# The gate stores of the last built tile, issued on GpSimd's queue

## The chip, the cores and the metric

The kernel runs on one core of a Trainium2 chip. The metric is the device time of one launch in microseconds (us). PE is the matrix engine, DVE VectorE, ACT ScalarE, POOL GpSimd; SP is the engine that here only issues DMAs. Each engine runs its own list of instructions strictly in order; they meet through semaphores only. A DMA is issued by one engine, in that engine's order, and lands later.

## The reference, cut to what matters

One layer of an encoder trunk over 1024 tokens of width 1024, in float32: two kinds of attention, a projection, a layer norm, and then a PEER block, whose output goes through a second layer norm.

```
q   = x @ w_q                                  # 8 heads x 2 halves x 128
sc  = einsum(q, sub_keys)                      # 8 x 2 x 128 scores a token
s_top, i_top = top_k(sc, 16)                   # per half
cand = s_top[0][:, None] + s_top[1][None, :]   # 16 x 16 sums a head
fs, fpos = top_k(cand, 16)
eidx = the 16 expert numbers of a head (of 16384);  g = softmax(fs)
h   = x . u[eidx];   a = gelu(h) * g;   out = sum a * v[eidx]
```

So each token uses 128 experts of 16384, each with a gate g.

## The kernel before

Tokens stand in eight tiles (t = 0 to 7) of 128. Tiles 0 to 4 (`ND = 5`) are done densely: all 16384 experts are computed for them on PE, and a table of gates, mostly zeros, masks the result. Tiles 5 to 7 fetch the rows of their experts (`gather_gen`, L659, indirect DMAs on POOL).

The gate table of the dense tiles is made in two ways. For tiles 0 and 1 (`NS = 2`), `scatter` (L165) issues 256 indirect DMAs on POOL, each adding 128 gates into `gs` in DRAM. For tiles 2 to 4, `build` makes the table with one-hot products: for each of four quarters of 32 tokens there are eight steps, in each of which DVE compares (`pi` L605, `qj` L609), ACT scales `qj` by the gate (L614), PE multiplies (`pr`, L618) and ACT copies the product into the tile `stage` (L619). After eight steps the quarter, 2 MB, is stored to `gd` by one DMA (L620). The pool r1 holds `stage` with `bufs=1`: there is one buffer, and the first copy of a quarter waits until the store of the quarter before has landed.

The program is built in this order: projections, attention and `route(0)` (tiles 0 and 1, with all the scatters), then three rounds of attention of two tiles, with one `build(1)` after the attention of a tile while something is left to build, and `route(pr)`. `route` projects with w_q (16 steps c: loads `kt`, `qhi`, `qlo` on SP; PE `pq`; ACT copies `q` L562 and `sc` L567; DVE `top16`), and then `decode` on DVE finds expert numbers and gates. Tile 4 is routed in `route(2)`, so its build stands in the last round, after the attention of tile 6. The tile framework's scheduler then orders each engine's instructions by its own model of time; the four quarters of tile 4 come out interleaved with the steps of `route(3)` on ACT, DVE and PE.

After that the dense stage runs: 128 expert blocks e, with loads `gt` (gates, L703 from `gs` and L708 from `gd`), `raw` (L712, L730) on SP, the products `h` (L91 to L93), `po` and `fl` on PE, and the gathers of tiles 5 to 7 between them. The first `gt` load waits for every scatter and every store to `gd`.

Of the kernel before, what the change touches and what calls it, by code (L numbers as in the profile page):

```python
# [21 lines left out]
P = 128  # L22
# [15 lines left out]
ND = 5  # L38
NG = NT - ND
DN = ND * P  # L40
GC = 32
NS = 2
# [15 lines left out]
def trunk(ctx, tc, x, xt, wqk, wo, gn, sink, biasa, biasb, ln, wq, keyst, uv, ut, vt, out):  # L58
    nc = tc.nc
# [53 lines left out]
    gd = tc.dram_tile([(ND - NS) * P // GC, P, P, GC], F32, name="gd")  # L113
# [126 lines left out]
    with ExitStack() as att:  # L240
# [344 lines left out]
        def build(n):  # L585
            for t, idx, g in todo[:n]:
                ij = rb.tile([P, 2, P], F32, name="ij", bufs=1)
                tmp = rb.tile([P, 2, P], I32, name="ijt", bufs=1)
                nc.vector.tensor_scalar(tmp[:, 0, :], idx, 7, None, op0=OP.logical_shift_right)
                nc.vector.tensor_scalar(tmp[:, 1, :], idx, 127, None, op0=OP.bitwise_and)  # L590
                nc.vector.tensor_copy(ij, tmp)
                pt = ps_r.tile([P, 4, P], F32, name="pr")
                nc.tensor.transpose(pt[:, 0, :], ij[:, 0, :], ident)
                nc.tensor.transpose(pt[:, 1, :], ij[:, 1, :], ident)
                nc.tensor.transpose(pt[:, 2, :], g, ident)
                tt = rb.tile([P, 3, P], F32, name="tt", bufs=1)
                nc.scalar.copy(tt, pt[:, 0:3, :])
                for q in range(P // GC):
                    stage = r1.tile([P, P, GC], F32, name="stage")
                    for s in range(GC // 4):  # L600
                        ps = ps_r.tile([P, 4, P], F32, name="pr")
                        pi = rb.tile([P, 4, P], F32, name="pi")
                        tok0 = q * GC + s * 4
                        io4 = iota[:, None, :].to_broadcast([P, 4, P])
                        nc.vector.tensor_tensor(pi, io4, tt[:, 0, tok0:tok0 + 4, None].to_broadcast([P, 4, P]),  # L605
                                                OP.is_equal)
                        qj = rb.tile([P, 4, P], F32, name="qj")
                        if s % 4 < GACT:
                            nc.vector.tensor_tensor(qj, io4, tt[:, 1, tok0:tok0 + 4, None].to_broadcast([P, 4, P]),  # L609
                                                    OP.is_equal)  # L610
                        for c in range(4):
                            tok = tok0 + c
                            if s % 4 < GACT:
                                nc.scalar.activation(qj[:, c, :], qj[:, c, :], AF.Copy, scale=tt[:, 2, tok:tok + 1])  # L614
                            else:
                                nc.vector.tensor_scalar(qj[:, c, :], iota, tt[:, 1, tok:tok + 1],
                                                        tt[:, 2, tok:tok + 1], op0=OP.is_equal, op1=OP.mult)
                            nc.tensor.matmul(ps[:, c, :], qj[:, c, :], pi[:, c, :], start=True, stop=True)  # L618
                        nc.scalar.copy(stage[:, :, 4 * s:4 * s + 4].rearrange("p i c -> p c i"), ps)  # L619
                    nc.sync.dma_start(gd[(t - NS) * (P // GC) + q], stage)  # L620
            del todo[:n]

        route(0)
        for pr in range(1, 4):
            for t in (2 * pr, 2 * pr + 1):
                att_head(t)
                att_main(t)
                build(1)
            att_out(2 * pr)
            route(pr)  # L630
# [235 lines left out]
```

## Time and profile before

| | us |
|---|---|
| median of 3 runs | 3006.41 (3004.22 to 3008.86) |
| the profiled execution: its time | 3008.4 |
| its span, first to last instruction | 3006.6 |
| scatters on POOL, first to last issue | 608.3 to 1128.7 |
| stores of tile 4's four quarters, issued on SP | 1059.27, 1084.81, 1114.30, 1135.54 |
| first `gt` load issued | 1142.00 |
| dense stage | about 1160 to the end |

Times in the trace count from the start of the span. A row of the chain or of a timeline gives start and duration in us, what ran, and in brackets how long the engine was idle before it and what ended that. The windows view gives the busy time of each engine in a stretch, the granted TensorE clock (1.00 is 2.4 GHz, 0.50 is 1.2 GHz), the busy share of the DMA engines and the rate they moved.

### The profile page before, as it was taken

Reading aid. Unit: us, or ns where it says so; the run is one execution under the profiler, and the core shown is the slowest. Engines: PE = TensorE matmul, PEld = TensorE weight load, DVE = VectorE, ACT = ScalarE, POOL = GpSimd, SP = SyncE. Lnnn points to the kernel's source line nnn. Section 1 sums busy time; section 2 is a strip of 40 time slices with the busy share of each in tenths; the row PEclk is TensorE's granted clock in tenths of the full one; section 3 lists DMA queues with packets and bytes.
Section 4 is the critical chain, followed back from the end, with each engine's and each line's share of the span. In section 5 each row is a group of like instructions: output and inputs, shape, how many; then the busy total and the mean of one; then the engine's idle time right before and its main releaser. Section 6 shows DMA issues by size and latency. Waiting matters only on the chain.

```text
span 3006.6 us, 43280 instructions
## 1 busy us (share of the span) xinstructions
PE 2803.2 (93%) x15569; PEld 2379.3 (79%) x15569; DVE 2412.6 (80%) x5427; ACT 1201.7 (40%) x2486; POOL 1085.2 (36%) x748
## 2 busy tenths in 40 slices
PE   6998899998998785999999999999999999999997
PEld 5766567575785775898898889989889899889885
DVE  3343267887988978898998998999999889989975
ACT  2344155242686672333333333333333333333332
POOL 1211001078888881233333333333333333333310
PEclk8999989799899797999999999999999999999998
DMA  7798588796887675998999989999999899899861
GB/s 239 214 269 264 188 298 284 239 268 153 243 231 227 176 212 201 337 341 317 335 343 331 333 328 343 335 346 330 332 342 346 292 352 339 323 339 359 325 245 49
DMA packets 384119, 854.43 MB, mean 284 GB/s; under 512 B 90016, under 2 KB 241568, under 8 KB 332960
## 3 DMA queue, kind: packets, MB, share of 16 engines
q0 software_dynamic: 132672, 437.68, 42.0%
q1 hardware_dynamic: 221600, 384.62, 37.6%
q10 hardware_dynamic: 29632, 29.37, 3.3%
q8 instruction: 122, 2.00, 0.3%
q14 instruction: 93, 0.76, 0.1%
HBM read 761.01 MB, written 90.31 MB: 283 GB/s over the span
## 4 chain that ended last, share of the span: by engine, by line
PE 72%; DMA 11%; DVE 9%; ACT 5%; issue 3%; POOL 1%; SPq 0%; ACTq 0%; DVEq 0%; POOLq 0%
PE h L91 9%; PE h L92 9%; PE h L93 9%; PE po L739 5%; PE po L740 5%; PE po L741 5%; PE fl L739 3%; PE fl L740 3%; PE fl L741 3%; PE ps L486 3%; PE y L362 2%; PE pq L558 2%; PE pr L618 2%; DMA gd<-stage 1%; PE pq L559 1%
## 5 line engine op out<-in xcount | busy, mean ns | idle before, releaser
L659 POOL DMA_INDIRECT uv<-in_uv_dram,eidx x384 | 572.6, 1491 | 1184.8 <-DVE acc L671 755.7
L91 PE MATMUL h<-dh,uh 128*128 128x320 f32 x2048 | 639.9, 312 | 45.1 <-ACT gl L721 22.5
L93 PE MATMUL h<-dh,ul 128*128 128x320 f32 x2048 | 634.6, 310 | 0.4 <-DVE ul L87 0.4
L92 PE MATMUL h<-dl,uh 128*128 128x320 f32 x2048 | 634.1, 310 | 0.0
L165 POOL DMA_INDIRECT gs<-gated,idxd x256 | 440.3, 1720 | 169.0 <-DMA qlo<-wqd 86.7
L661 DVE SCALAR_TENSOR_TENSOR uv<-uv,xg 128x1024 f32<-128x1024 f32 x384 | 467.0, 1219 | 41.9 <-DMA uv<-in_uv_dram,eidx 41.8
L671 DVE SCALAR_TENSOR_TENSOR acc<-uv,hh,acc 128x1024 f32<-128x1024 f32 x381 | 487.7, 1280 | 3.7
L91 PEld LDWEIGHTS h<-dh,uh 128*128 128x128 f32 x2048 | 386.1, 189 | 76.4 <-ACT gl L721 43.8
L92 PEld LDWEIGHTS h<-dl,uh 128*128 128x128 f32 x2048 | 386.2, 189 | 11.4
L93 PEld LDWEIGHTS h<-dh,ul 128*128 128x128 f32 x2048 | 386.1, 189 | 3.3 <-DVE ul L87 0.8
L739 PE MATMUL po<-vh,ah 128*128 128x512 f32 x768 | 288.4, 391 | 0.5 <-ACT ah L86 0.5
L740 PE MATMUL po<-vl,ah 128*128 128x512 f32 x768 | 287.6, 390 | 0.0
L741 PE MATMUL po<-vh,al 128*128 128x512 f32 x768 | 260.9, 391 | 0.0
L767 ACT COPY fl<-fl 128x512 f32<-128x512 f32 x252 | 147.1, 584 | 277.2 <-PE fl L741 276.8
L665 ACT ACTIVATE hh<-hh 128x1 f32<-128x1 f32 x384 | 77.6, 202 | 435.4 <-DVE uv L661 434.2
L721 ACT ACTIVATE gl<-h 128x320 f32<-128x320 f32 x256 | 111.5, 436 | 284.0 <-PE h L93 282.2
L768 DVE TENSOR_TENSOR facc<-facc,fl 128x512 f32<-128x512 f32 x252 | 173.1, 687 | 63.8 <-ACT fl L767 62.8
L739 PE MATMUL fl<-vh,ah 128*128 128x512 f32 x512 | 202.2, 395 | 6.5 <-ACT fl L767 4.3
L740 PE MATMUL fl<-vl,ah 128*128 128x512 f32 x512 | 202.1, 395 | 0.0
L741 PE MATMUL fl<-vh,al 128*128 128x512 f32 x512 | 200.0, 391 | 0.0
L87 DVE TENSOR_TENSOR ul<-raw,uh 128x1024 fp32r<-128x1024 f32 x128 | 156.2, 1220 | 49.6 <-ACT uh L86 48.8
L86 ACT CAST uh<-raw 128x1024 fp32r<-128x1024 f32 x128 | 134.2, 1048 | 122.5 <-PE h L92 71.7
(201 smaller groups left out, 5454.0 us busy)
## 6 DMA issues: line engine op xcount, KB each, us to landing
raw<-in_ut_dram SPq DMA_DIRECT2D x128, 512.0 KB
raw<-in_vt_dram SPq DMA_DIRECT2D x128, 512.0 KB
qhi<-wqd SPq DMA_DIRECT2D x48, 512.0 KB
qlo<-wqd SPq DMA_DIRECT2D x48, 512.0 KB
gd<-stage SPq DMA_DIRECT2D x12, 2048.0 KB
gt<-gd SPq DMA_DIRECT2D x32, 768.0 KB
wraw<-in_wqk_dram SPq DMA_DIRECT2D x36, 512.0 KB
bt<-in_biasb_dram SPq DMA_DIRECT2D x64, 288.0 KB
```

Source lines behind the costliest of these rows:

```text
L87: nc.vector.tensor_sub(lo, raw, f(hi))
L91: nc.tensor.matmul(ps, wh, mh, start=first, stop=False)
L92: nc.tensor.matmul(ps, wh, ml, start=False, stop=False)
L93: nc.tensor.matmul(ps, wl, mh, start=False, stop=last)
L165: st = nc.gpsimd.indirect_dma_start(out=gs, out_offset=bass.IndirectOffsetOnAxis(ap=idx[:, k:k + 1], axis=0), in_=g[:, k:k + 1], in_offset ...
L659: nc.gpsimd.indirect_dma_start(out=u, out_offset=None, in_=uv, in_offset=bass.IndirectOffsetOnAxis(ap=eidx[t][:, k:k + 1], axis=0))
L661: nc.vector.scalar_tensor_tensor(u[:, 0:D], u[:, 0:D], 1.0, x1[t], op0=OP.mult, op1=OP.mult, accum_out=hh[:, k:k + 1])
L671: nc.vector.scalar_tensor_tensor(acc, u[:, D:], hh[:, k:k + 1], acc, op0=OP.mult, op1=OP.add)
L739: nc.tensor.matmul(ps, ah[:, cs], vh[:, js], start=first, stop=False)
L740: nc.tensor.matmul(ps, ah[:, cs], vl[:, js], start=False, stop=False)
L741: nc.tensor.matmul(ps, al[:, cs], vh[:, js], start=False, stop=last)
L768: nc.vector.tensor_add(acc[:, j, :], acc[:, j, :], fl)
```

## The change

The store of each quarter is issued by `nc.gpsimd` where the tile is the last dense one (t = 4), and by `nc.sync` as before for tiles 2 and 3. Nothing else is edited.

```
-                    nc.sync.dma_start(gd[(t - NS) * (P // GC) + q], stage)
+                    (nc.gpsimd if t == ND - 1 else nc.sync).dma_start(gd[(t - NS) * (P // GC) + q], stage)
```

On POOL, around the end of the scatters and the first gather of tile 5, there stood before (`gated`, `idxd` are the gates and places of tile 1, `uv` a fetched row; DMASW names a semaphore of POOL's DMAs, DMAHW one of SP's and ACT's):

```order
L165 DMA gs_97<-gated_3589,idxd_3588 4194304x1 [waits DMASW1_49]
L165 DMA gs_97<-gated_3589,idxd_3588 4194304x1 [waits DMASW2_49]
L165 DMA gs_97<-gated_3589,idxd_3588 4194304x1 [waits DMASW3_49]
L659 DMA uv_11517<-in_uv_dram,eidx5_102 128x2048 [waits DMASW7_49,DMAHW0_49,DMASW6_49,DMAHW1_49,DMASW5_49,DMAHW2_49,DMASW4_49,DMAHW3_49,DMASW3_49,DMAHW4_49,DMASW2_49,DMAHW5_49,DMASW1_49,DMAHW6_49,DMASW0_49,DMAHW7_49,DVE_49,PE_49]
L659 DMA uv_11523<-in_uv_dram,eidx5_102 128x2048
```

and now, at the same place:

```order
L165 DMA gs_97<-gated_3589,idxd_3588 4194304x1 [waits DMASW1_49]
L165 DMA gs_97<-gated_3589,idxd_3588 4194304x1 [waits DMASW2_49]
L165 DMA gs_97<-gated_3589,idxd_3588 4194304x1 [waits DMASW3_49]
L620 DMA gd_98<-stage_9379 128x4096 [waits DMASW4_49,Activation_49]
L620 DMA gd_98<-stage_9493 128x4096 [waits DMASW5_49,Activation_49]
L620 DMA gd_98<-stage_9607 128x4096 [waits DMASW6_49,Activation_49]
L620 DMA gd_98<-stage_9721 128x4096 [waits DMASW7_49,Activation_49]
L659 DMA uv_11517<-in_uv_dram,eidx5_102 128x2048 [waits DMAHW1_49,DMAHW2_49,DMAHW0_49,DMAHW3_49,DMASW3_49,DMAHW4_49,DMASW2_49,DMAHW5_49,DMASW1_49,DMAHW6_49,DMASW0_49,DMAHW7_49,DVE_49,PE_49]
L659 DMA uv_11523<-in_uv_dram,eidx5_102 128x2048
```

The four stores stand on POOL behind the last of the 256 scatters and ahead of the first gather.

On ACT, at the turn from the first to the second quarter of tile 4 (`stage_9379` is the first quarter, `stage_9493` the second; `q` and `sc` belong to `route(3)`), there stood before:

```order
L562 COPY q_10723<-pq_10698 128x256 [waits PE_49]
L567 COPY sc_10728<-pq_10725 128x256 [waits PE_49]
L614 ACTIVATE qj_9539<-qj_9539,tt_9377 128x128 [waits DVE_49]
L614 ACTIVATE qj_9539<-qj_9539,tt_9377 128x128 x3
L619 COPY stage_9493<-pr_9494 128x4x128 [waits DMAHW5_49]
L619 COPY stage_9493<-pr_9508 128x4x128
L562 COPY q_10773<-pq_10748 128x256 [waits PE_49]
L619 COPY stage_9493<-pr_9522 128x4x128 [waits PE_49]
```

and now:

```order
L562 COPY q_10723<-pq_10698 128x256 [waits PE_49]
L567 COPY sc_10728<-pq_10725 128x256 [waits PE_49]
L614 ACTIVATE qj_9539<-qj_9539,tt_9377 128x128 [waits DVE_49]
L614 ACTIVATE qj_9539<-qj_9539,tt_9377 128x128 x3
L619 COPY stage_9493<-pr_9494 128x4x128 [waits DMASW4_49]
L619 COPY stage_9493<-pr_9508 128x4x128
L562 COPY q_10773<-pq_10748 128x256 [waits PE_49]
L619 COPY stage_9493<-pr_9522 128x4x128 [waits PE_49]
```

No row moved there; only the semaphore that the first copy of the second quarter waits on is another, that of the store on POOL. The same holds at the turns to the third and fourth quarter. On SP the four rows of L620 are gone, and the loads around them keep their order. From the last steps of tile 4's build on, the scheduler has put rows of DVE, ACT and PE in a slightly different order, and so in the dense stage, where for instance the `po` and `fl` products change places with `h` products.

## Rows read from the trace of the kernel before

**Rows 1.** Windows: engines' busy us, counts, clock, DMA share, GB/s.

```profile
core 0: us, PE busy (x) PEld busy (x) DVE busy (x) ACT busy (x) POOL busy (x), PEclk, DMA share, GB/s
...
1121.00:1135.00 14.00, 8.49 (x48) 7.40 (x48) 14.00 (x91) 11.97 (x24) 8.59 (x5) 0.85 0.15 1
1135.00:1142.00 7.00, 0.00 (x0) 0.00 (x0) 7.00 (x48) 0.82 (x2) 0.00 (x0) 0.50 0.71 300
1142.00:1160.00 18.00, 2.71 (x9) 2.31 (x10) 18.00 (x87) 3.33 (x4) 0.00 (x0) 0.50 0.83 243
1160.00:1190.00 30.00, 24.81 (x142) 22.53 (x142) 27.77 (x63) 8.91 (x12) 1.45 (x1) 0.97 0.39 124
1190.00:1250.00 60.00, 57.19 (x311) 51.29 (x310) 46.22 (x68) 17.02 (x35) 15.84 (x14) 0.97 0.95 356
1250.00:2000.00 750.00, 742.05 (x4131) 670.55 (x4130) 684.73 (x999) 270.01 (x542) 254.60 (x168) 1.00 0.91 334
2000.00:2950.00 950.00, 939.45 (x5229) 846.77 (x5228) 851.76 (x1236) 342.15 (x681) 300.72 (x202) 1.00 0.88 322
```

**Rows 2.** The chain that ended last, 1056 to 1101: start, us, what.

```profile
1059.27 8.16 DMA gd<-stage
1067.44 0.47 issue
1067.91 1.98 ACT stage L619 x2
...
1084.81 11.24 DMA gd<-stage
1096.08 1.02 ACT stage L619
```

**Rows 3.** Timeline of POOL, 1057 to 1190.

```profile
1057.50 2.02 POOL L165 DMA_INDIRECT gs<-gated,idxd  x1 [0.30 <-issue]
1059.83 1.55 POOL L165 DMA_INDIRECT gs<-gated,idxd  x1 [0.30 <-issue]
...
1128.69 2.12 POOL L165 DMA_INDIRECT gs<-gated,idxd  x1 [0.30 <-issue]
1188.32 1.45 POOL L659 DMA_INDIRECT uv<-in_uv_dram,eidx  x1 [57.52 <-PE h L93]
```

**Rows 4.** Timeline of ACT, turns to the second and fourth quarter.

```profile
1067.91 1.07 ACT L619 COPY stage<-pr 128x512 f32<-128x512 f32 x1 [0.72 <-DMA gd<-stage]
...
1120.46 0.37 ACT L567 COPY sc<-pq 128x256 f32<-128x256 f32 x1 [0.80 <-PE pq L565]
1120.75 1.93 ACT L619 COPY stage<-pr 128x512 f32<-128x512 f32 x2
```

**Rows 5.** Timeline of SP: first, third and fourth store, first gt load.

```profile
1059.27 0.42 SPq L620 DMA_DIRECT2D gd<-stage  x1
...
1114.30 0.32 SPq L620 DMA_DIRECT2D gd<-stage  x1
...
1135.54 0.32 SPq L620 DMA_DIRECT2D gd<-stage  x1
1142.00 0.37 SPq L703 DMA_DIRECT2D gt<-gs  x1
```

**Rows 6.** Timeline of POOL: two of its plain stores, 256 and 512 KB.

```profile
105.52 0.80 POOL L305 DMA_DIRECT2D kd<-sh  x1 [6.08 <-ACT sh L86]
...
356.13 0.53 POOL L552 DMA_DIRECT2D wqd<-qlo  x1
```

**Rows 7.** The chain: the first gather of 1 MB on POOL's queue.

```profile
1188.32 8.24 DMA uv<-in_uv_dram,eidx
```

**Rows 8.** Waits of SP, 1110 to 1150: us in total, times, longest.

```profile
SPq L620 <- ACT stage L619: 20.9, 1, 20.9
SPq L620 <- ACT q L562: 6.3, 1, 6.3
SPq L703 <- DMA gd<-stage: 5.6, 1, 5.6
```

**Rows 9.** PE's h products, 1142 to 1200: ns min/median/max.

```profile
L93 PE MATMUL h<-dh,ul x48: 303/309/637, 1158.2 to 1196.3; 128*128 128x320 f32 x48
```

## The prediction

> **What bounds the kernel now.** I read the windows first, to see which stage could move at all. From about 1160 us to 2950 us PE is busy for nearly all of each stretch: it is idle for 5.2, 2.8, 8.0 and 10.6 us in the four windows, 26.5 us together [rows 1]. The dense stage is thus bound by PE's work, and whatever delays its start delays the end by the same amount; at most 26.5 us of idle time could be given back there. The change sits ahead of that stage, so the question is when the stage starts. I then read the chain that ended last, backwards from there. From 1121 to 1160 DVE is busy in every microsecond (14.00, 7.00 and 18.00 us in windows of those lengths) with the last top-16 and the decoding of tiles 6 and 7 [rows 1]. That work cannot begin before the last score copy, `sc`, which ACT makes at 1120.46 [rows 4]. Before that point the chain hops between ACT's `stage` copies and the stores of `gd`: the store issued at 1059.27 is followed by the copy at 1067.91, and the one issued at 1084.81 takes 11.24 us, until the copy at 1096.08 [rows 2]. So the single `stage` buffer, and the landing of the store that empties it, sit on the path already. ACT runs in order, and the `q` and `sc` copies of `route(3)` stand behind those `stage` copies; when a store is late, the routing of tiles 6 and 7 is late with it, and not only the gate table.
>
> Last I read POOL over the same stretch, because that is where the stores go. POOL issues scatters without a gap: each takes about 1.55 us plus 0.30 us, the one that is running when the first quarter is ready (1057.50 to 1059.52) is followed by 37 more, the first at 1059.83 and the last at 1128.69, which ends at 1130.81; then POOL has nothing to do until the first gather at 1188.32 [rows 3].
>
> **The change part by part.** *Removed from SP*: four issues of 0.32 to 0.42 us [rows 5]. SP is not what the engines wait for here: it stood 6.3 and 20.9 us at the third and fourth store because the quarter was not ready, and what is queued behind these is the next store and then the `gt` loads, which need that store anyway [rows 8]. The loads of `kt`, `qhi` and `qlo` keep their places and wait for their buffers. Removing the issues is worth nothing on the path.
>
> *Added to POOL: the first store.* Its place is behind all 256 scatters. The quarter is ready at about 1059.1, as before (SP issues the store at 1059.27 [rows 5]), but POOL comes to it at 1128.69 + 2.12 + 0.30 = 1131.1 [rows 3]. What is behind it: on POOL the other three stores and the first gather, which does not run before 1188 in any case; on ACT the first copy of the second quarter, and behind that everything else on ACT. PE then fills its buffers `pr` and `pq` and stops; DVE fills `pi` and `qj` and stops; SP fills `qhi`, `qlo` and `kt` and stops. There is one or two steps of slack in this and no other work: the attention is over, the decoding of tiles 4 and 5 too, and the dense stage's loads stand behind the `gt` loads.
>
> The store's own time on POOL's queue isn't in the trace. The nearest row is the fourth store on SP, issued at 1135.54 with the `gt` load that waits for it at 1142.00, 6.46 us, with the DMA engines at 300 GB/s and next to nothing else running [rows 1, 5]; in the stalled program as little else will run. A plain store costs POOL 0.53 to 0.80 us to issue against SP's 0.32 [rows 6], so I add 0.5 us and take 7.0. The lower bound is 6.5. The upper bound is the one row of POOL's queue with a landing: a gather of 1 MB that took 8.24 us beside three more gathers, doubled for 2 MB to 16.5 [rows 7]. I am much nearer the lower one, since that gather shared the engines.
>
> So the second quarter's first copy comes at 1131.1 + 7.0 = 1138.1 in place of 1067.91: **+70.2 us**. Less contention should let the 37 scatters run closer to 1.85 us each, 68.5 us where they took 71.3 (1059.83 to 1131.1 [rows 3]); I take off about half of the difference, **-1 us**, bounds 0 and -2.8.
>
> *Added to POOL: the other three stores.* POOL is free by then, so each goes when its quarter is ready, with 0.5 us more to issue. The second is waited for on ACT in full. The third is not: ACT finishes `sc` at 1120.46 and goes on at 1120.75 without an idle row, so it landed in time [rows 4]. The fourth is waited for by the `gt` load only, while DVE decodes. On the path: **+1 us**; bounds 0, and up to 5 us each for three stores if POOL's queue lands 2 MB as slowly as [rows 7] says in part.
>
> *PE's clock.* Where PE stands idle in the old trace the granted clock is 0.50 (1135 to 1160), and afterwards 0.97 [rows 1]; at the lower level an `h` product takes 637 ns in place of 309 [rows 9]. After a stall of 70 us the first microseconds of PE's work should run at the lower level. I take it that some 4 us of PE's work at the restart run at half the pace, with ACT's copies and DVE's compares beside it: **+2 us**, a choice, with bounds 0 and 5. A step of slack in the filled buffers gives back **-1 us**, bounds 0 and -3.
>
> *The moved rows of the dense stage.* The order of `po`, `fl` and `h` products changes, their number does not. PE is over 98% busy in the long windows, so I take 0; it can't give back more than 26.5 us [rows 1], and I allow a quarter of that each way.
>
> **Sum.** 70.2 - 1 + 1 + 2 - 1 = +71.2 us, everything from the second quarter on shifted by one amount. The profiled execution took 3008.4 us for a span of 3006.6, so it would become 3079.6; the median of the runs is 2 us below it, so the median after is 3006.4 + 71.2 = 3077.6, say **3078 us**. The bounds of the terms: at the low end 1131.1 - 2.8 + 6.5 - 1067.9 = 66.9, less 3 and less 7 gives +57; at the high end 9.5 for the first store, some 10 for the others, 3 for the clock and 7 for the dense stage on top of 71 give about +100, but not all at once; I cut that to +95.
>
> **A rule that speaks the other way.** The rows say that the issuing queue decides, because what stands ahead on it is 71 us long. The Trainium skill, Trainium Kernel Development and Optimization, section Key Constraints, says that DMAs issued from the SP, ACT and POOL queues all run on the same 16 DMA engines and interleave, and that issuing from several engines only saves the sequencer's issue time. By that rule alone the change would be worth four issue slots and nothing else; it is the second rival below. No run here yet shows which holds for these stores; the rule is about DMAs that have been issued, while this one waits its turn on POOL.
>
> **Rivals.** *1. Slower by more: POOL's queue lands 2 MB slowly.* If each of the four took the 16.5 us of the doubled gather [rows 7], the first adds 9.5, the second about 5 over its 11.24 [rows 2], the third and fourth up to 10 each, since they stop being hidden: 3078 + 35 = 3113 us. For it: the queue's only measured landing. Against: that one ran among others.
>
> *2. The other side, no stall.* The stores leave when their quarter is ready, because POOL is through with its scatters by then. Then ACT goes on at 1067.9 as today, and the `gt` load might leave up to 5.6 us earlier [rows 8] if it no longer stood behind SP's fourth store, while 0.5 us an issue is lost; as DVE is busy to 1160 anyway, the time is 3001 to 3007 us. It decides at 1059.3: the 37 scatters that run after that would all have to be gone, or stand behind the stores. Against: the order on POOL puts all of them ahead, and their pace is set by their own 1.85 us, which nothing in this change shortens.
>
> *3. Slower by less: the dense stage gives time back.* If the new order filled all of PE's 26.5 us of idle time [rows 1], the time would be 3078 - 26 = 3052 us. Against: nothing in the change makes its inputs arrive sooner.
>
> **How the numbers follow.** The forecast, a stall of about 70 us that nothing hides, has a chance of 0.86, with 3063 to 3101 us around 3078. Rival 1 beyond 3101 has 0.07, rival 2 has 0.04, rival 3 below 3063 has 0.03. The range 3063 to 3101 leaves these three out, 0.14 together. A measurement of this kernel can tell about 0.2%, 6 us, from no change. Faster by more than that and within it come from rival 2 alone, 0.01 and 0.03; slower has 0.96.
>
> **What would show it.** In the trace after, POOL should have its last scatter at about 1128, and the first `gd` store right behind it at 1130 to 1131. ACT should stand idle from about 1067 to 1137, with the store of `gd` as the releaser, in one wait of about 70 us, and the chain should show one `gd` row of that length or POOL's scatters in its place. PE and DVE should be nearly empty in 1070 to 1137, and PE's clock 0.50. The last `sc` copy should come at about 1191 in place of 1120.5, the first `gt` load at about 1213, and from there to the end the trace should be as long as before (1864.6 us from the first `gt` load). The prediction is wrong if POOL issues the first store before 1100, if ACT does other work during the wait, or if the stretch from the first `gt` load to the end differs by more than 7 us.

## The result and the profile after

The changed kernel takes 3077.7 us in the median of four runs (3075.9 to 3086.44) against 3005.31 of the kernel before on the same chip (2998.56 to 3008.86): 72.4 us more. The ratio is 1.0258, with a 95% interval of 1.0234 to 1.0282. The forecast was 3078, slower. The profiled execution took 3086.44 us for a span of 3084.7, 9 us more than the median. Three launches far out of line (6156.69 and 12539.0 us of the kernel before beside e1 to e4, 14938.85 us of e5) are left out of the times below.

POOL's timeline after, around the end of the scatters (start and duration in us, operation, idle before it and what ended it), to be read against [rows 3]:

```profile
1057.85 2.01 POOL L165 DMA_INDIRECT gs<-gated,idxd  x1 [0.30 <-issue]
...
1129.12 1.55 POOL L165 DMA_INDIRECT gs<-gated,idxd  x1 [0.31 <-issue]
1130.09 1.19 POOL L620 DMA_DIRECT2D gd<-stage  x1
1156.15 0.57 POOL L620 DMA_DIRECT2D gd<-stage  x1 [24.86 <-ACT q L562]
1182.56 0.53 POOL L620 DMA_DIRECT2D gd<-stage  x1 [25.84 <-ACT q L562]
1206.26 0.53 POOL L620 DMA_DIRECT2D gd<-stage  x1 [23.16 <-ACT gate L231]
1256.09 1.00 POOL L659 DMA_INDIRECT uv<-in_uv_dram,eidx  x1 [49.30 <-PE h L93]
```

The first store leaves right behind the last scatter. ACT had filled that quarter at 1057.6. The other three leave when they are ready, with POOL idle before each. ACT's timeline in the same stretch, to be read against [rows 4]:

```profile
1056.54 1.03 ACT L619 COPY stage<-pr 128x512 f32<-128x512 f32 x1
...
1064.44 1.28 ACT L614 ACTIVATE qj<-qj,tt 128x128 f32<-128x128 f32 x4
1137.30 1.88 ACT L619 COPY stage<-pr 128x512 f32<-128x512 f32 x2 [71.58 <-DMA gd<-stage]
...
1165.46 1.91 ACT L619 COPY stage<-pr 128x512 f32<-128x512 f32 x2 [3.05 <-DMA gd<-stage]
...
1188.47 0.37 ACT L567 COPY sc<-pq 128x256 f32<-128x256 f32 x1 [0.80 <-PE pq L565]
1189.14 1.91 ACT L619 COPY stage<-pr 128x512 f32<-128x512 f32 x2 [0.29 <-DMA gd<-stage]
```

One wait of 71.58 us stands where there was one of 0.72 in [rows 4]. The windows view (us, busy us and count of PE, PE's loads, DVE, ACT and POOL, granted clock, DMA share, GB/s) shows what the other engines do in it:

```profile
core 0: us, PE busy (x) PEld busy (x) DVE busy (x) ACT busy (x) POOL busy (x), PEclk, DMA share, GB/s
1059.00:1068.00 9.00, 7.82 (x62) 7.22 (x60) 7.29 (x36) 4.26 (x14) 7.47 (x6) 1.00 0.64 170
1068.00:1130.00 62.00, 0.00 (x0) 0.00 (x0) 0.00 (x0) 0.00 (x0) 51.93 (x34) 0.52 0.26 17
1130.00:1138.00 8.00, 0.00 (x0) 0.00 (x0) 0.00 (x0) 0.70 (x1) 1.28 (x2) 0.50 0.68 262
1138.00:1142.00 4.00, 3.63 (x17) 3.63 (x18) 1.29 (x2) 2.44 (x4) 0.00 (x0) 0.50 0.02 4
1142.00:1146.00 4.00, 3.16 (x25) 2.97 (x25) 3.73 (x18) 3.62 (x10) 0.00 (x0) 0.98 0.06 16
```

PE, DVE and ACT do not one instruction between 1068 and 1130; only POOL works. PE starts again with a granted clock of 0.50 and has 0.98 four microseconds later. On SP the first `gt` load, at 1142.00 in [rows 5], is now at

```profile
1213.23 0.37 SPq L703 DMA_DIRECT2D gt<-gs  x1
```

71.2 us later. And the chain that ended last, by engine and line, now has POOL's scatters in it:

```profile
PE 44%; POOL 14%; issue 7%; DVE 6%; DMA 6%; ACT 1%; ACTq 0%; POOLq 0%; DVEq 0%
POOL gs L165 13%; PE h L91 8%; PE h L92 7%; PE h L93 7%; PE po L739 4%; PE po L740 4%; PE po L741 4%; DMA uv<-in_uv_dram,eidx 3%; PE fl L739 3%; PE fl L740 3%; PE fl L741 3%; DMA raw<-in_ut_dram 2%; DVE uv L661 2%; DVE acc L671 1%; POOL uv L659 1%
```

Before, POOL had 1% of the chain and the scatters were not in it. The 13% of the scatters is 400 us and not 71: followed backwards, the chain reaches the first store on POOL and then walks the scatters, one issued behind the other. It shows what the store stands behind, not what the change costs.

### The profile page after: what moved, and what is told of

Read it like the earlier page. It is cut to its first block, busy times and chain, and to the rows that moved or that the text cites. A ratio compares the mean times of both kernels' runs of the same rounds, so it can differ in the third digit from the quotient of the medians.

```text
span 3084.7 us, 43277 instructions
## 1 busy us (share of the span) xinstructions
PE 2804.4 (91%) x15569; PEld 2378.8 (77%) x15569; DVE 2412.7 (78%) x5427; ACT 1202.2 (39%) x2486; POOL 1091.2 (35%) x752
## 4 chain that ended last, share of the span: by engine, by line
PE 44%; POOL 14%; issue 7%; DVE 6%; DMA 6%; ACT 1%; ACTq 0%; POOLq 0%; DVEq 0%
POOL gs L165 13%; PE h L91 8%; PE h L92 7%; PE h L93 7%; PE po L739 4%; PE po L740 4%; PE po L741 4%; DMA uv<-in_uv_dram,eidx 3%; PE fl L739 3%; PE fl L740 3%; PE fl L741 3%; DMA raw<-in_ut_dram 2%; DVE uv L661 2%; DVE acc L671 1%; POOL uv L659 1%
## 5 line engine op out<-in xcount | busy, mean ns | idle before, releaser
L659 POOL DMA_INDIRECT uv<-in_uv_dram,eidx x384 | 581.2, 1513 | 1170.7 <-DVE acc L671 719.3
L618 PE MATMUL pr<-pi,qj 128*128 128x128 f32 x768 | 129.2, 312 | 104.3 <-ACT stage L619 78.1
L618 PEld LDWEIGHTS pr<-pi,qj 128*128 128x128 f32 x768 | 115.2, 217 | 117.9 <-ACT stage L619 79.6
```

The lines of the kernel that those rows point to most:

```text
L659: nc.gpsimd.indirect_dma_start(out=u, out_offset=None, in_=uv, in_offset=bass.IndirectOffsetOnAxis(ap=eidx[t][:, k:k + 1], axis=0))
```

## The experiments

The theory: the store of a quarter waits on POOL until the last scatter has been issued, and ACT, which needs the one `stage` buffer, waits with it. The rivals: a store of 2 MB on POOL's queue costs by itself; leaving SP costs by itself; or the other order of rows that the scheduler made costs. All times stand against the kernel before, timed beside them on the same chip: 3004.12 us (e1 to e4), 3006.4 (e5 to e8) and 3005.26 (e9).

**e1, e2, e3: one quarter after the other back on SP.** With n = 0, 1 and 2 (... stands for the rest of the line):

```
-(nc.gpsimd if t == ND - 1 else nc.sync).dma_start(gd...
+(nc.gpsimd if t == ND - 1 and q > n else nc.sync).dma_start(gd...
```

> Only the first quarter of tile 4 is stored from SP, as before; the other three stay on POOL behind the scatters. Theory (a store waits on POOL until the last scatter is through, at about 1130.7 in the trace after, and its landing about 6.6 us later frees ACT's stage buffer): the wait moves to the first copy of the third quarter, which comes at 1137.3 in place of 1096.1 in the trace of before, +41 us: 3005 + 41 + 1 = 3047 us. Rival, each store costs by itself on POOL's queue (72 us for four, 18 each): three stores give +54, 3059 us. Rival, what costs is the other order of the rows that comes with the change: the same as the changed kernel, 3078 us.

> The first two quarters from SP, the last two on POOL. Theory: the wait is at the first copy of the fourth quarter, at 1137.3 in place of 1120.75, +16.6 us: 3023 us. Rival, a price for each store on POOL's queue: two stores, +36, 3041 us. Rival, the order of the rows: 3078 us.

> Only the fourth quarter on POOL. Its store is ready at about 1135.5 in the trace of before, after the last scatter (1130.8). Theory: no wait is left, +0 to +2 us: 3005 to 3008 us. Rival, a price for each store: +18, 3023 us. Rival, the order of the rows: its order differs from that of before about as much as the changed kernel's, so 3078 us.

Measured: e1 3051.12 us (ratio 1.0151, 1.0108 to 1.0194), e2 3027.62 (1.0076, 1.0048 to 1.0104), e3 3019.25 (1.0039, 1.002 to 1.0058). The long wait of ACT is, in e1 and then in e2,

```profile
1126.64 1.88 ACT L619 COPY stage<-pr 128x512 f32<-128x512 f32 x2 [47.08 <-DMA gd<-stage]
```

```profile
1133.74 1.87 ACT L619 COPY stage<-pr 128x512 f32<-128x512 f32 x2 [22.94 <-DMA gd<-stage]
```

the first at the turn to the third quarter and the second at the turn to the fourth, as the theory has it. Waits of 71.58, 47.08 and 22.94 us go with 72.4, 47.0 and 23.5 us of time. A price per store would have given 54 and 36; the order of the rows alone, 72 each time, and on ACT, DVE and PE e1 and e2 have the rows of the changed kernel.

Both waits are some 6 us longer than the shifts that I expected, for two different reasons. In e1 a part of the wait is not new, since ACT waited at this turn before as well:

```profile
1096.08 1.87 ACT L619 COPY stage<-pr 128x512 f32<-128x512 f32 x2 [4.73 <-DMA gd<-stage]
```

So 42.4 us are new, against 41 expected; e1's time is 5 us above that, inside its interval (32 to 58 us). In e2 I had taken the moment at which ACT needs the buffer from the one trace of before: ACT came to the fourth quarter at 1110.80 (1133.74 - 22.94) in place of 1120.75, 10 us sooner, while the scatters ended only 3.7 us sooner (1127.10 against 1130.81).

e3 did not come out as any of them said. ACT's wait at the fourth quarter is gone, and the first `gt` load is no later than in [rows 5]:

```profile
1139.43 0.37 SPq L703 DMA_DIRECT2D gt<-gs  x1
```

Yet it is 15.1 us slower in the medians, 12 us by the ratio. The stretch from that load to the end is 1877.9 us (span 3017.3) against 1864.6. That is taken up in e9. A small wait on POOL was left too: the fourth quarter is full at 1127.91, and its store goes out at 1131.89 with the end of the last scatter, so that the `gt` load comes 11.5 us after the quarter is full, where it is 7.2 us in e4. "No wait is left" was 4 us short.

**e4: the four stores on ACT's queue.** `nc.gpsimd` becomes `nc.scalar`. DVE, PE and POOL keep the rows of the kernel before in their order.

> All four stores of tile 4 issued by ACT, right behind the copy that fills the quarter; nothing else moves. Theory (what stands ahead on the issuing queue decides): nothing stands ahead there that the store has to wait for, so no stall; ACT issues four more DMAs: 3003 to 3008 us. Rival, taking the stores off SP costs by itself (loads of the routing that now run ahead of them on SP take their share of the DMA engines): +72 or a good part of it.

Measured: 3001.37 us, ratio 0.9995 (0.9976 to 1.0014), no difference that can be told. The stores are issued at once:

```profile
1048.15 0.34 ACTq L620 DMA_DIRECT2D gd<-stage  x1
1074.15 0.33 ACTq L620 DMA_DIRECT2D gd<-stage  x1
1103.97 0.33 ACTq L620 DMA_DIRECT2D gd<-stage  x1
1125.34 0.33 ACTq L620 DMA_DIRECT2D gd<-stage  x1
```

So leaving SP costs nothing. What costs is where the stores go.

**e5 and e6: half of the scatters, stores on POOL and on SP.**

```
-            for h in range(8):
+            for h in range(4):
                 for t, idx, g in dense:
                     scatter(t, h, idx, g)
-        for b in added[t, 7]:          # in load_g
+        for b in added[t, 3]:
```

> The changed kernel with scatters for four of the eight heads only (128 in place of 256; the gates of heads 4 to 7 of tiles 0 and 1 are left out of the table). All four stores are still on POOL, and the rows of ACT, DVE and PE stand in the order of the changed kernel. Theory: the scatters end at about 608 + 128 x 2.04 = 869 us, before the first quarter is ready, so each store leaves when it is ready and the stall of 71 us is gone: within 8 us of e6, about 3000 to 3010. Rival, POOL's queue is slow for each 2 MB: the 72 us stay, 3078. Rival, the other order of the dense stage costs part of the 72: that part stays as the distance from e6.

> The control of e5: the same 128 scatters (the same gates left out), all stores on SP and the order of rows of the kernel before. Theory: the scatters were not on the path before, so 2998 to 3006 us; a few us less than before if the scatters' share of the DMA engines slowed the other transfers.

Measured: e5 3007.01 us (1.0014, 0.9995 to 1.0033), e6 3000.95 (0.9992, 0.9974 to 1.001). POOL has issued its last scatter at 859 us in e5. The four stores are on POOL as in the changed kernel, and they do no harm:

```profile
1050.84 0.60 POOL L620 DMA_DIRECT2D gd<-stage  x1 [190.22 <-ACT qj L614]
1076.46 0.57 POOL L620 DMA_DIRECT2D gd<-stage  x1 [25.02 <-ACT q L562]
1102.78 0.53 POOL L620 DMA_DIRECT2D gd<-stage  x1 [25.75 <-ACT q L562]
1124.87 0.53 POOL L620 DMA_DIRECT2D gd<-stage  x1 [21.56 <-ACT stage L619]
```

The rival of a slow queue is out. What lies between e5 and e6, 6 us in the medians, is all that POOL's queue and the other order of the rows can cost together; the two intervals overlap, so these times alone do not show that it is anything.

**e7: seven eighths of the scatters.** As e5, with `range(7)` and `added[t, 6]`.

> The changed kernel with scatters for seven of eight heads (224; the gates of head 7 of tiles 0 and 1 are left out). Theory: 32 fewer scatters at 1.85 to 2.04 us let POOL come to the first store 59 to 65 us sooner, at 1066 to 1072, so that the second quarter's first copy comes at 1072 to 1078 in place of 1067.9: +4 to +10 us, 3009 to 3016 us. Rival, a price for each store on POOL's queue: 3078 us as the changed kernel.

Measured: 3024.25 us, 1.0077 (1.005 to 1.0104), 17.9 us over the kernel before and 8 more than the upper end of what I expected.

```profile
1068.28 1.55 POOL L165 DMA_INDIRECT gs<-gated,idxd  x1 [0.30 <-issue]
1069.25 1.19 POOL L620 DMA_DIRECT2D gd<-stage  x1
```

```profile
1076.46 1.89 ACT L619 COPY stage<-pr 128x512 f32<-128x512 f32 x2 [12.21 <-DMA gd<-stage]
```

The first fence is POOL's timeline, the second ACT's. The copy comes at 1076.46, inside the 1072 to 1078 that I gave; but I set that against the 1067.91 of [rows 4], and in e1 to e4 the same copy comes between 1056.04 and 1060.49. Against those it is 16 to 20 us late. Of that 12.2 us are the wait, and the rest is that in this execution the first quarter was full only at 1056.10, against 1047 to 1052 in e1 to e4. The second quarter then took 18.4 us to fill where it took 17.0 in e1 to e3, with a granted clock of 0.50 from 1076 to 1080. What else is in the 17.9 us isn't shown. The dose is as the theory wants it: 128, 224 and 256 scatters give a longest wait at this place of nothing, 12.2 and 71.6 us.

**e8: the changed kernel again.**

> The changed kernel once more, for a second profile. In its first profile the stretch from the first gt load to the end was 1871.5 us long against 1864.6 before, 6.9 us more. If that is the moved rows of the dense stage, it comes again, and e5 is about 7 us over e6; if it is this one execution, the stretch is 1858 to 1867 us here, and the whole 3075 to 3079 us.

Measured: 3075.56 us, 1.0247 (1.0223 to 1.0272), 69.2 us over the kernel before. ACT's wait is 73.42 us, the first `gt` load comes at 1208.13, and the stretch from there to the end (span 3073.8) is 1865.7 us. So the 6.9 us that this stretch had over that of before in the first profile do not come again in full: 1.1 us are left.

**e9: what made e3 slow.** e3 with half of the scatters, so that POOL is free; PE, DVE, ACT and SP have the same rows in the same order as in e3.

```
e5's edit, and
+(nc.gpsimd if t == ND - 1 and q > 2 else nc.sync).dma_start(gd...
```

> e3 (only the fourth quarter on POOL) with 128 scatters in place of 256 (the gates of heads 4 to 7 of tiles 0 and 1 are left out). PE, DVE, ACT and SP have the same rows in the same order as in e3; POOL is free from about 860 us on. e3 was 13 us over the kernel before, with its first gt load no later (1139.4 against 1142.0) and the stretch from there to the end 1877.9 us against 1864.6. Theory, the order of the dense stage's rows costs those 13 us: they stay, 3012 to 3017 us against 3001 for e6, and the stretch is 1873 to 1880 us. Rival, the wait on POOL's queue at the fourth store costs them: 3000 to 3004 us and a stretch of 1863 to 1868.

Measured: 3018.92 us, 1.0046 (1.0024 to 1.0067), 2 us above the upper end of what I expected. The first `gt` load and a span of 3020.7 give a stretch of 1884.3 us, 4 above the upper end.

```profile
1136.38 0.37 SPq L703 DMA_DIRECT2D gt<-gs  x1
```

The store leaves at 1129.40, 0.3 us after its quarter is full, so 13.7 us over the kernel before are there without any wait on POOL. Nor is it a store on POOL by itself, since e5 has four of them and no such loss. The order of the rows is left, which e3 and e9 share and no other version here has. PE's waits from 1130 to 3030 (us in total, times, longest) say where, in the kernel before, in e3 and in e9:

```profile
PE h L91 <- ACT gl L721: 22.5, 28, 2.5
```

```profile
PE h L91 <- ACT gl L721: 34.3, 42, 4.0
```

```profile
PE h L91 <- ACT gl L721: 36.5, 43, 4.1
```

In that order an `h` product waits 42 or 43 times, not 28, for ACT to empty the one PSUM tile. That accounts for 12 to 14 us, the size of the loss in the times; the stretch of the one e9 profile is 19.7 us longer than that of before, and the other 6 us of it stay open. Why ACT comes later in that order isn't shown either.

No version beat the kernel before: e4 is its equal within the interval.

## Why the prediction was right, point by point

- **Where the store would leave.** 1131.1 forecast, less 1 for faster scatters, and it left with the end of the last scatter, at 1129.12 + 1.55 = 1130.7. The mechanism is right, but two errors in its size cancel, which is luck. In the trace of before 36 scatters follow the one that was running, not the 37 of the prediction, at 1.98 us each; after, they ran at 1.87 us, near the 1.85 forecast, and 36 of them at that pace save 4 us, not 1. But 39 stood ahead of the store, since in that execution the scatters began 4.4 us later (612.63 against 608.26) and the quarter was full 1.5 us sooner. e7 shows that the scatters set it: 32 fewer of them, and the store leaves 61 us sooner (1069.3 against 1130.1).
- **The landing on POOL's queue.** 7.0 us were taken, between 6.5 and 16.5. From 1130.7 to ACT's copy at 1137.30 it is 6.6 us, from 1182.56 to 1189.14 6.6, from 1206.26 to the `gt` load 7.0, and 9.3 for the second, which shares the DMA engines and took 11.24 in [rows 2]. Rival 1, POOL's queue slow by itself, is refuted by these rows and by e5.
- **The stall.** +69.2 (70.2 less 1) forecast, 1137.30 - 1067.91 = 69.4 measured, with nothing beside it on PE, DVE or ACT.
- **The clock and the slack.** +2 and -1 forecast. From ACT's first copy of the second quarter to its store it takes 1156.15 - 1137.30 = 18.9 us, where it took 16.9, and PE's granted clock is 0.50 in the first 4 us: +2.0 for the two together. No run parts the one from the other.
- **The other stores.** +1 was taken, and -0.1 came: the second landed 1.9 us faster, the third quarter took 1.1 less to fill and the fourth 2.3 more, with 0.6 more for the landing of the last two. To the first `gt` load the sum of all terms is 71.2 both in the forecast and in the trace. That the last digit agrees is chance: the moment at which the first quarter is full moves by up to 12 us between the eleven traces (1047.3 to 1059.0), which I hadn't allowed for.
- **The moved rows of the dense stage.** 0 was taken, with 7 either way. The stretch from the first `gt` load to the end is 1871.5 and 1865.7 us in two profiles of the changed kernel, and 1869.3, 1867.1, 1870.7 and 1869.2 in e1, e2, e5 and e7, which have its rows on ACT, DVE and PE: 1868.9 in the mean. In the order of before it is 1864.6, 1868.8 (e4) and 1863.1 (e6), 1865.5 in the mean. 3 us between the two stay open: they are of the size of the scatter. The allowance was too small for such a change all the same: e3's order, from a change of one quarter's queue, cost 12 to 15. Rival 3, time given back by this stage, is refuted: none of these stretches in the new order is shorter than the 1864.6 us of the trace of before.
- **Rival 2, no stall**, came true where its condition was met: in e5, with the scatters gone by 861 us (3007.01 us, against its 3001 to 3007).
- **The rule on queues.** These rows first: four stores issued on ACT cost nothing, the same four on POOL behind scatters 72 us, on POOL without scatters nothing that can be told. The Trainium skill, Trainium Kernel Development and Optimization, section Key Constraints, has it that DMAs of all queues share the 16 engines and that another issuing engine only saves issue time. For e4 and e5 that holds; as a forecast of the changed kernel's time it doesn't, since it says nothing of what stands ahead of a DMA on its own engine.

## What to carry to other kernels

Before a DMA is moved to another engine's queue, look at what that engine still has to issue when the data is ready: here 39 indirect DMAs of 1.87 us each, 72.8 us, and ACT waited 71.6. Then look who waits for the buffer: a store that frees a single buffer stops the engine that fills it, and with in-order issue everything queued behind that copy, here the routing of two more tiles. No run gives `stage` a second buffer, so how much of the wait that would take away isn't shown. With a scheduler between the source and the program, a one-line edit also reorders stages far away, and that alone was worth some 14 us here; a control with the same order tells it apart.

## What was not expected

An order of PE's and ACT's rows that a scheduler chose after an edit of one store's queue cost 12 to 15 us in the dense stage (e3, and again 13.7 in e9), with PE's waits for `gl` going from 22.5 to 34.3 and 36.5 us. And the moment at which the first quarter is full differs by 12 us between the eleven traces, so that a moment read from one trace is not good to the microsecond; the whole time of the kernel before moves by 23 us between its runs beside e5 to e8 (2994.44 to 3017.23).
